# A diagonal prefix-sum kernel: more row sums on VectorE, and sixteen input rows loaded at the start

## The chip, the cores and the metric

One core of one Trainium2 chip. The metric is the device time of one execution in microseconds (us), the median over several runs. Most runs of one kernel agree within 0.3%. A version counts as the same within 2%.

## The reference

```python
def setup_inputs():
    B, H, W = 4, 4224, 4224
    return {"x": np.random.randn(B, H, W).astype(np.float32)}

def reference(x):
    ps = np.cumsum(np.cumsum(x, axis=1), axis=2)
    diag = np.diagonal(ps, axis1=1, axis2=2)
    return np.cumsum(diag, axis=1).astype(np.float32)
```

Only the diagonal of the two-dimensional prefix sum is wanted, summed up along itself. Each element of the input is needed once, as a part of a column sum or of a row sum.

## The kernel before

GpSimd issues the loads of "strips" of 768 rows, which convert fp32 to bf16 on the way. There are three strip buffers. VectorE masks the diagonal block and sums the row parts to its left; PE adds up the columns to the right, in groups of 384, six matmuls a group. For some groups VectorE adds the six rows of each partition first (`by_rows`), and PE needs one fp32 product, which it runs as two matmuls.

```python
    NBUF = 3
    ...
    head = last.tile([P, 2, HC], FP32, name="head")
    nc.sync.dma_start(out=head, in_=src_a[:, :, N - HC : N])
    ...
    for i in range(NBUF):                      # three strips on the way at once
        t = strip_tile()
        load_rows(t, 0, i * F2 * P)            # nc.gpsimd.dma_start
        prefetched.append(t)
    ...                                        # constants
    row_sums(hs[:, 0:2], head)                 # VectorE, head rows of the last batch
    ...
        def add_up(strip, f, r0, acc, um, wp=0, ws=None, by_rows=False):
            ...
            nc.vector.tensor_mul(out=mu, in0=block, in1=um)
            nc.vector.tensor_sub(out=block, in0=block, in1=mu)
            if by_rows:
                rowed = mup.tile([P, GW], FP32, name="rowed")
                row_sums(rowed, strip[:, :, hi : hi + GW].rearrange("p q c -> p c q"))
            ...                                # PE: columns of mu, product of rowed
            row_sums(acc[:, :, 1], strip[:, :, ws:hi])
```

The last 128 rows of the last batch come at the end, in four blocks of 32 rows; the last block comes in two pieces, and the sums over it end the kernel.

## Time and profile before

| | before |
|---|---|
| median of the three runs at hand | 668.94 us (667.32 to 669.8) |
| span of the profiled run | 665.6 us |
| VectorE busy | 380.8 us (57%) |
| PE busy | 206.6 us (31%) |
| from a strip load's issue to its landing | 72.6 us (median of 19) |

The span is the time from the first to the last instruction of the profiled run; the device time is some 2 us more. A row of section 5 of the page reads: line, engine, operation, what it writes from what it reads, count, then busy time and mean, then the engine's idle time just before and what ended it.

### The profile page before, as it was taken

Reading aid. Unit: us, or ns where it says so; the run is one execution under the profiler, and the core shown is the slowest. Engines: PE = TensorE matmul, PEld = TensorE weight load, DVE = VectorE, ACT = ScalarE, POOL = GpSimd, SP = SyncE. Lnnn points to the kernel's source line nnn. Section 1 sums busy time; section 2 is a strip of 40 time slices with the busy share of each in tenths; the row PEclk is TensorE's granted clock in tenths of the full one; section 3 lists DMA queues with packets and bytes.
Section 4 is the critical chain, followed back from the end, with each engine's and each line's share of the span. In section 5 each row is a group of like instructions: output and inputs, shape, how many; then the busy total and the mean of one; then the engine's idle time right before and its main releaser. Section 6 shows DMA issues by size and latency. Waiting matters only on the chain.

```text
span 665.6 us, 2495 instructions
## 1 busy us (share of the span) xinstructions
PE 206.6 (31%) x948; PEld 94.1 (14%) x948; DVE 380.8 (57%) x176; ACT 136.1 (20%) x219; POOL 31.3 (5%) x59
## 2 busy tenths in 40 slices
PE   0071522302117143140211723404031363350418
PEld 0030211100003021010000311201000131120103
DVE  3161828476946173756794526466589433352766
ACT  0001121406300103040630020304063002030434
POOL 7000000000000000000000000000000000001000
PEclk9995857656558585665655857657565585776758
DMA  9999999999999999999999999999999999999998
GB/s 203 219 219 219 219 219 218 218 209 210 219 220 219 218 220 219 218 216 215 209 219 219 219 216 219 219 218 216 213 213 219 219 216 216 219 218 218 215 206 162
DMA packets 7672, 143.23 MB, mean 215 GB/s; under 512 B 704, under 2 KB 1004, under 8 KB 2156
## 3 DMA queue, kind: packets, MB, share of 16 engines
q0 software_dynamic: 7296, 142.47, 99.9%
q1 hardware_dynamic: 364, 0.61, 0.3%
q8 instruction: 7, 0.11, 0.1%
q14 instruction: 5, 0.04, 0.0%
HBM read 285.47 MB, written 0.07 MB: 429 GB/s over the span
## 4 chain that ended last, share of the span: by engine, by line
DVE 54%; another core or an unknown queue 37%; DMA 5%; PE 3%; issue 1%; DVEq 0%; POOLq 0%
DVE acc L258 28%; DVE mu L351 8%; DVE strip L352 8%; DVE rowed L258 7%; DMA strip<-in_x_dram 5%; DVE c L481 1%; PE d L211 1%; PE fold L218 0%; PE d L218 0%; DVE pu L258 0%; DVE c L278 0%; DVE rows L403 0%; DVE acc L376 0%; PE fold_a L218 0%
## 5 line engine op out<-in xcount | busy, mean ns | idle before, releaser
L253 ACT ACTIVATE dump<-strip 128x416 bf16<-128x416 bf16 (+6 forms) x108 | 124.4, 1151 | 520.2 <-DMA strip<-in_x_dram 517.5
L351 DVE TENSOR_TENSOR mu<-strip,um 128x4608 bf16<-128x4608 bf16 (+1 forms) x24 | 52.4, 2184 | 260.4 <-DMA strip<-in_x_dram 260.3
L258 DVE TENSOR_REDUCE acc<-strip 128x6 f32<-128x4608 bf16 (+6 forms) x23 | 195.9, 8518 | 0.4
L218 PEld LDWEIGHTS <-sel 128*11 128x11 bf16 x643 | 66.7, 104 | 482.5 <-issue 453.6
L211 PE MATMUL d<-strip,sel 128*11 128x384 bf16 x90 | 37.3, 415 | 295.8 <-DMA strip<-in_x_dram 295.8
L218 PE MATMUL d<-strip,sel 128*11 128x384 bf16 x441 | 116.6, 408 | 0.0
L352 DVE TENSOR_TENSOR strip<-strip,mu 128x4608 bf16<-128x4608 bf16 (+1 forms) x24 | 52.4, 2183 | 1.0
L211 PE MATMUL d<-mu,sel 128*11 128x384 bf16 x43 | 16.3, 379 | 108.5 <-DVE mu L351 108.5
L258 DVE TENSOR_REDUCE rowed<-strip 128x384 f32<-128x2304 bf16 x12 | 49.0, 4082 | 0.0
L218 PE MATMUL d<-mu,sel 128*11 128x384 bf16 x200 | 46.7, 369 | 0.0
L76 POOL DMA_DIRECT2D strip<-in_x_dram x24 | 16.4, 686 | 542.7 <-DVE acc L258 292.8
L253 ACT ACTIVATION_READ_ACCUMULATOR dump<-strip 128x1 f32 x108 | 20.1, 186 | 0.0
L211 PE MATMUL d<-rowed,sel_f 128*11 128x384 f32 x24 | 11.5, 566 | 20.3 <-DVE rowed L258 20.3
L211 PEld LDWEIGHTS <-sel 128*11 128x11 bf16 x134 | 13.6, 102 | 19.3 <-issue 12.3
L211 PE MATMUL d<-ident,rows 128*11 128x128 f32 x24 | 5.2, 379 | 16.8 <-DVE rows L412 16.8
L258 DVE TENSOR_REDUCE pu<-d 11x1 f32<-11x384 f32 x4 | 2.2, 545 | 6.3 <-PE d L211 6.3
L94 DVE MEMSET um<- 128x4608 bf16 (+1 forms) x2 | 4.9, 2458 | 1.1 <-issue 1.1
L95 POOL TENSOR_SCALAR_AFFINE_SELECT um<-um 128x4608 bf16<-128x4608 bf16 (+1 forms) x2 | 5.2, 2612 | 2.6 <-DVE um L94 2.6
L211 PE MATMUL d<-halves,rows 128*11 128x64 f32 x48 | 5.3, 288 | 0.0
L211 PEld LDWEIGHTS d<-ident,rows 128*11 128x11 f32 x24 | 2.5, 118 | 18.9 <-DVE rows L412 11.7
L211 PEld LDWEIGHTS d<-rowed,sel_f 128*11 128x11 f32 x24 | 1.5, 91 | 24.9 <-DVE rowed L258 24.6
L211 PEld LDWEIGHTS d<-halves,rows 128*11 128x11 f32 x48 | 4.8, 128 | 1.4 <-issue 1.3
(102 smaller groups left out, 60.6 us busy)
## 6 DMA issues: line engine op xcount, KB each, us to landing
strip<-in_x_dram POOLq DMA_DIRECT2D x19, 6336.0 KB, 72.6
strip<-in_x_dram POOLq DMA_DIRECT2D x5, 3168.0 KB, 55.8
strip<-in_x_dram POOLq DMA_DIRECT2D x1, 1080.0 KB, 49.9
strip<-in_x_dram POOLq DMA_DIRECT2D x1, 768.0 KB, 52.9
strip<-in_x_dram POOLq DMA_DIRECT2D x3, 256.0 KB, 54.1
head<-in_x_dram SPq DMA_DIRECT2D x1, 528.0 KB, 3.8
strip<-in_x_dram POOLq DMA_DIRECT2D x1, 192.0 KB, 43.2
strip<-in_x_dram POOLq DMA_DIRECT2D x1, 64.0 KB, 28.5
```

The source lines that it names most:

```text
L76: nc.gpsimd.dma_start(out=o, in_=x[b, r0 : r0 + f * P, :].rearrange("(p f) w -> p f w", f=f))
L94: nc.vector.memset(um, 1.0)
L95: nc.gpsimd.affine_select(out=um, in_=um, compare_op=ALU.is_gt, fill=0.0, base=0, pattern=[[-1, f], [1, f * P]], channel_multiplier=-f,)
L211: nc.tensor.matmul(o, lhsT=lhsT, rhs=rhs, start=start, stop=False, skip_group_check=True)
L218: te.add_instruction(mybir.InstMatmult(start_tensor_calc=False, stop_tensor_calc=False, tile_position=(0, 0), tile_size=(P, P if lhsT.shap ...
L253: nc.scalar.activation(out=dump[:, :w], in_=src, func=ACT.Copy, accum_out=acc)
L258: nc.vector.reduce_sum(out=acc, in_=src, axis=AX.X)
L351: nc.vector.tensor_mul(out=mu, in0=block, in1=um)
L352: nc.vector.tensor_sub(out=block, in0=block, in1=mu)
L481: nc.vector.tensor_tensor_scan(out=c12[:, i, :], data0=ones_row, data1=src, initial=carry[:, i : i + 1], op0=ALU.mult, op1=ALU.add,)
```

## The change

The intent: take matmuls away from PE (50 groups summed on VectorE in place of 12), and shorten the end (the last 16 rows loaded at the start on SyncE's queue, behind the head and apart from the strips' queue, so that the last block has 16 rows; the 10-row store issued after a more urgent one).

```diff
+    NE = 8
+    EK = P // NE
+    EB = N - 2 * NE
+    early = last.tile([P, 2, TB // EK], FP32, name="early")
+    for h in range(2):
+        nc.sync.dma_start(
+            out=early[:, h, :],
+            in_=x[LB, EB + h * NE : EB + (h + 1) * NE, :TB].rearrange(
+                "r (k c) -> r k c", k=EK
+            ),
+        )
     ... (weights for 8 and 16 pieces a row; one "pair" tile in place of several)
+    earlysum = last.tile([P, 2], FP32, name="earlysum")
+    row_sums(earlysum, early)                  # before the loop over the batches
     ...
-            if by_rows:
-                rowed = mup.tile([P, GW], FP32, name="rowed")
-                row_sums(rowed, ...)
+            def over_rows(j0, j1):
+                rowed = mup.tile([P, 2 * GW], FP32, name="rowed")
+                ... (one reduce for two groups, then one product a group)
-                strip, F2, s * F2 * P, acc6[:, s], um6, by_rows=whole and s > 0
+            by_rows = (4, 4, 3, 2, 1) if whole else (4, 4, 0, 0, 0)
     ...
-                (3, 0, bcut),                  # last block: 32 rows, 4 pieces a row
-                (3, bcut, CB),
+                (3, RL, 8, 0, bcut),           # last block: 16 rows, 8 pieces a row
+                (3, RL, 8, bcut, CL),
     ...
+        matmul(fin_e, earlysum[:, 0:1], weights16, start=True)
+        matmul(fin_e[:, NE:], earlysum[:, 1:2], weights16[:, : R - NE])
     ...
+        store_groups()                         # the 10-row store, now after the first yl store
```

More of the change, by code (lines that the diff above doesn't have):

```diff
@@ L198, with row_weights @@
     R = P // 4
-    steps = consts.tile([P, P], I32, name="steps")
-    nc.gpsimd.iota(steps, pattern=[[4, P]], base=7, channel_multiplier=-1)
-    nc.vector.tensor_single_scalar(
-        out=steps, in_=steps, scalar=2, op=ALU.arith_shift_right
-    )
-    weights4 = consts.tile([P, P], FP32, name="weights4")
-    nc.vector.tensor_scalar_max(out=weights4, in0=steps, scalar1=0.0)
+    RL = R - 2 * NE
+    def row_weights(shift, width, skip=0):
+        k = 1 << shift
+        steps = consts.tile([P, P], I32, name="steps")[:, :width]
+        nc.gpsimd.iota(
+            steps,
+            pattern=[[k, width]],
+            base=2 * k - 1 - k * skip,
+            channel_multiplier=-1,
+        )
+        nc.vector.tensor_single_scalar(
+            out=steps, in_=steps, scalar=shift, op=ALU.arith_shift_right
+        )
+        w = consts.tile([P, width], FP32, name=f"weights{k}")
+        nc.vector.tensor_scalar_max(out=w, in0=steps, scalar1=0.0)
+        return w
+    weights4 = row_weights(2, P)
+    weights8 = row_weights(3, R)
+    weights16 = row_weights(4, R, RL)
     ident_h = consts.tile([P, P], BF16, name="ident_h")
@@ L264, in pair_sum @@
         w = src.shape[-1] // 2
-        pair = last.tile([P, 288], FP32, name=f"pair{len(pairs)}")
-        pairs.append(pair)
+        if not pairs:
+            pairs.append(last.tile([P, 288], FP32, name="pair"))
+        pair = pairs[0]
         nc.vector.scalar_tensor_tensor(
@@ L336, in columns, with add_up @@
             first[0] = False
-        def add_up(strip, f, r0, acc, um, wp=0, ws=None, by_rows=False):
+        def add_up(strip, f, r0, acc, um, wp=0, ws=None, by_rows=0):
             nw = f * P // GW
@@ L352, in add_up @@
             nc.vector.tensor_sub(out=block, in0=block, in1=mu)
-            if by_rows:
-                rowed = mup.tile([P, GW], FP32, name="rowed")
-                row_sums(
-                    rowed,
-                    strip[:, :, hi : hi + GW].rearrange("p q c -> p c q"),
-                )
             for h in range(nw):
@@ L361, in add_up @@
                     columns(g + h, 0, GW, mu[:, q, h * GW : (h + 1) * GW], q > 0)
-            if by_rows:
-                k = row_of(g + nw)
-                matmul(d, sel_f[:, NG - 1 - k : 2 * NG - 1 - k], rowed)
+            def over_rows(j0, j1):
+                rowed = mup.tile([P, 2 * GW], FP32, name="rowed")
+                n = (j1 - j0) * GW
+                row_sums(
+                    rowed[:, :n],
+                    strip[:, :, j0 * GW : j1 * GW].rearrange("p q c -> p c q"),
+                )
+                for j in range(j0, j1):
+                    k = row_of(j)
+                    matmul(
+                        d,
+                        sel_f[:, NG - 1 - k : 2 * NG - 1 - k],
+                        rowed[:, (j - j0) * GW : (j - j0 + 1) * GW],
+                    )
+            j0, j1 = g + nw, g + nw + by_rows
+            jm = min(j0 + 2, j1)
+            if jm > j0:
+                over_rows(j0, jm)
             for q in range(f):
@@ L368, in add_up @@
             row_sums(acc[:, :, 1], strip[:, :, ws:hi])
+            if j1 > jm:
+                over_rows(jm, j1)
         acc6 = smalls.tile([P, NS, F2, 2], FP32, name="acc6")
@@ L385 @@
                 load_rows(strip, b, s * F2 * P)
-            add_up(
-                strip, F2, s * F2 * P, acc6[:, s], um6, by_rows=whole and s > 0
-            )
+            by_rows = (4, 4, 3, 2, 1) if whole else (4, 4, 0, 0, 0)
+            add_up(strip, F2, s * F2 * P, acc6[:, s], um6, by_rows=by_rows[s])
             if not whole and s == 0:
@@ L437 @@
             CB = TB // 4
-            bcut = 768
-            for sb, c0, c1 in (
-                (0, 0, CB),
-                (1, 0, CB),
-                (2, 0, CB),
-                (3, 0, bcut),
-                (3, bcut, CB),
+            CL = TB // 8
+            bcut = 256
+            for sb, r, k, c0, c1 in (
+                (0, R, 4, 0, CB),
+                (1, R, 4, 0, CB),
+                (2, R, 4, 0, CB),
+                (3, RL, 8, 0, bcut),
+                (3, RL, 8, bcut, CL),
             ):
@@ L448 @@
                     out=part_b[:, sb, c0:c1],
-                    in_=x[b, r0 : r0 + R, :TB].rearrange("r (k c) -> r k c", k=4)[
+                    in_=x[b, r0 : r0 + r, :TB].rearrange("r (k c) -> r k c", k=k)[
                         :, :, c0:c1
@@ L488, with store_groups @@
             )
-        j1 = NG - t0
-        nc.sync.dma_start(
-            out=out[b, : j1 * GW].rearrange("(g i) -> g i", i=GW),
-            in_=c12[t0:NG, 1, :],
-        )
+        def store_groups():
+            j1 = NG - t0
+            nc.sync.dma_start(
+                out=out[b, : j1 * GW].rearrange("(g i) -> g i", i=GW),
+                in_=c12[t0:NG, 1, :],
+            )
         if whole:
+            store_groups()
             continue
@@ L545 @@
         )
+        store_groups()
         act_sum(bsum[:, 1, 0:1], part_b[:, 2, :448])
@@ L549 @@
             weigh_b(bsum[:, 1, i : i + 1], weights4, 2 * R)
-        act_sum(esum[:, 0:1], part_b[:, 3, :320])
-        pair_sum(esum[:, 1:2], part_b[:, 3, 320:bcut])
-        pair_sum(esum[:, 2:3], part_b[:, 3, bcut:])
+        act_sum(esum[:, 0:1], part_b[:, 3, :96])
+        pair_sum(esum[:, 1:2], part_b[:, 3, 96:bcut])
+        pair_sum(esum[:, 2:3], part_b[:, 3, bcut:CL])
         nc.scalar.copy(out=yl[:, M0:], in_=fin_b)
@@ L559 @@
         for k in (1, 0, 2):
-            matmul(fin_e, esum[:, k : k + 1], weights4[:, :R], start=k == 1)
+            matmul(fin_e, esum[:, k : k + 1], weights8)
         nc.vector.tensor_add(out=ye, in0=fin_e, in1=yl[:, E0:])
```

## The prediction

> **What bounds the kernel now.** I read the profile from the whole to the end of the span: the page's shares, its DMA rows, the waits, the stretches between strip landings, the chain of waits, and last the DMA packet records.
>
> ```profile
> span 665.6 us, 2495 instructions
> PE 206.6 (31%) x948; PEld 94.1 (14%) x948; DVE 380.8 (57%) x176; ACT 136.1 (20%) x219; POOL 31.3 (5%) x59
> DMA  9999999999999999999999999999999999999998
> q0 software_dynamic: 7296, 142.47, 99.9%
> HBM read 285.47 MB, written 0.07 MB: 429 GB/s over the span
> L351 DVE TENSOR_TENSOR mu<-strip,um 128x4608 bf16<-128x4608 bf16 (+1 forms) x24 | 52.4, 2184 | 260.4 <-DMA strip<-in_x_dram 260.3
> ```
>
> No engine is busy for more than 57% of the span, the 16 DMA engines are busy in every slice, and VectorE's first operation on a strip has waited 260 us in all for the strip to land. The bytes read, 285.47 MB, are the whole fp32 input once (4 x 4224 x 4224 x 4 = 285.47 MB), so there is nothing to save in them. The stretches between landings say the same:
>
> ```profile
> core 0: us, PE busy (x) PEld busy (x) DVE busy (x) ACT busy (x) POOL busy (x), PEclk, DMA share, GB/s
> 64.50:95.30 30.80, 11.30 (x50) 5.16 (x50) 16.14 (x4) 3.84 (x12) 0.71 (x1) 0.67 0.98 211
> 95.30:125.20 29.90, 9.49 (x39) 4.00 (x39) 18.19 (x4) 6.10 (x12) 0.56 (x1) 0.61 1.01 217
> ```
>
> A strip of 768 rows is 768 x 4224 x 4 = 12.98 MB and lands every 29.9 us, 434 GB/s, while VectorE works 10 to 20 us of it. So only four things can move the time: the rate, the start before the queue is full, the finishing times of the 16 DMA engines, and what follows the last byte. The end, from the timeline:
>
> ```profile
> 648.81 0.56 PE L211 MATMUL fold<-strip,ident_h 128*128 128x480 bf16 x1 [10.68 <-DMA strip<-in_x_dram]
> ...
> 661.57 0.41 DVE L542 TENSOR_TENSOR yl<-fin_a,c 1x256 f32<-1x256 f32 x1 [0.56 <-PE fin_a L211]
> ...
> 662.35 0.39 DVE L267 SCALAR_TENSOR_TENSOR pair<-strip 128x224 f32<-128x224 bf16 x1
> 662.69 0.29 DVE L267 SCALAR_TENSOR_TENSOR pair<-strip 128x128 f32<-128x128 bf16 x1
> ...
> 663.41 0.18 DVE L561 TENSOR_TENSOR ye<-fin_e,yl 1x32 f32<-1x32 f32 x1 [0.41 <-PE fin_e L211]
> ```
>
> Two paths end together here. One is compute: from 648.81 the chain of waits runs without a gap through PE (fold), the scans and the corner sums to VectorE at 662.3. The other is DMA: in the packet records the last piece's final completion lands at 662.67, and the last pair sum starts at 662.69. From there it is 0.9 us to the last store's issue and 2 us for that store to finish.
>
> The packet records give one more thing. Each engine keeps an exact step of 29.893 us per strip, so a delay of one engine stays to the end. At the end seven engines finish at 661.3 to 661.65 and nine at 662.3 to 662.67. What made the nine late is mostly instruction fetches: seven packets of 16,384 B on the instruction queue q8, each of which pushed one engine back by about 1.1 us, and five of 8,192 B on q14 that pushed back by 0.3 to 0.5 us.
>
> **What the Trainium skill says.** "DMA: Bandwidth & Descriptors", Where 436 GB/s comes from: 16 ports give 435.2 GB/s. The trace agrees with 434 GB/s, so I count on no higher rate. The same page, Why a DMA increments its semaphore by 16 and not by 1: a hardware-queue DMA runs on the largest k up to 16 that divides the slowest dimension of both sides, on the lowest-numbered k engines. The trace agrees in count: the 10-row store is 10 packets of 1,536 B. So the early loads (8 rows each) run on engines 0 to 7. "Runtime: NRT & Kernel Launch", Instruction fetch mechanics: instructions are refilled in 16 KiB blocks of 256. The trace agrees: the seven fetches come 124 to 132 weight loads apart, each with its matmul. "VectorE: DVE Perf Modes", The perf-mode tier table: tensor_reduce has only the 1x mode. The trace shows worse for the row sum across the six rows: 2,304 elements take 4.07 us, against 4.95 us for 4,608 elements along the free axis.
>
> **Part one, 50 groups summed on VectorE** (12 now). The row "rowed" has 12 operations of 4,082 ns, so 38 more groups are 38 x 4.08 = 155 us: VectorE goes from 381 to some 536 us. PE loses 6 matmuls of about 408 ns a group and gains 2 of 490 ns: 38 x (6 x 0.408 - 2 x 0.49) = 56 us less. VectorE's fullest strip is the second of a batch: 2 x 2.57 (mask and subtract) + 7.06 (row sum) + 4 x 4.08 = 28.5 us, under 29.9. The first takes 26.4, the third 26.4, the fourth 24.7, the fifth is unchanged. After the fifth only 15 us pass until the 3-row strip, but the following strip gives 29.9 more, as now. So the waits for strips stay. A buffer is given back up to 16 us later, at about 27 us after its landing; it is needed when the two strips queued behind it are through, at 59.8 us. Some 30 us of slack remain, and the strip time does not move. This part is worth zero by itself except through instruction fetches: 38 x (6 - 2) = 152 pairs of weight load and matmul fewer, 4 more for the early rows, 948 - 152 + 4 = 800. Fetches now come at pairs 93, 221, ... 733, 861; at 800 pairs the seventh is gone. The sixth, now at 563 us, moves to the point where 64 pairs are left, which I count back to about 654 us.
>
> **Part two, the early loads.** 2 x 131,072 B over 8 engines is 32 packets of 1 KB an engine. Packets that read 1 KB follow each other every 40.5 ns in the tail, so 1.30 us an engine. Is that hidden at the start? The head's packets run from 2.2 to 4.5 us, and on each engine the first strip's packet follows the head's last within 0.01 us. There is no idle gap behind the head, so engines 0 to 7 start the strips 1.3 us later and carry that to the end.
>
> **Part three, the 16-row block.** Now an engine has 8 packets at 117 ns and 8 at 40.5 ns, 1.26 us; after it has 16 at 40.5 ns, 0.65 us. That takes 0.61 us from all 16 engines. Net: engines 8 to 15 are 0.6 us earlier, engines 0 to 7 are 0.7 us later.
>
> **Part four, the small ones.** The 10-row store goes out at about 662.3 in place of 659.91. Its packets came after each engine's last load packet anyway, so nothing is won, and its landing stays ahead of the last store's. The early rows' sum falls in VectorE's idle 14.8 us before the first strip. Their two products (0.3 us) fit before PE's wait for the scan.
>
> **The sum.** Which engines are the late ones? The 10-row store goes to engines 0 to 9, and its packets follow each engine's last completion: six of the seven early finishers are among them and four of the nine late ones. So mostly fast engines get the extra work, which looks like a balancing. A fast engine of 0 to 7 would end at 661.3 + 0.7 = 662.0, up to 662.35; late ones above 9 at 662.65 - 0.6 = 662.05. If nothing else hit them, the last byte would land at 662.3, 0.35 earlier than 662.67. But the sixth fetch, at 654, now falls into the tail. The sixth fetch hit an engine under 10 before; if it is one of 0 to 7 (I give it 0.6) that engine ends at 661.5 + 0.7 + 1.1 = 663.3, 0.65 later. Compute follows the half strip's landing at 648.8, which engines 0 to 7 may make later by 0 to 0.4 us; a shorter pair sum gives back 0.1. So compute allows a gain of 0.1 at most. Weighted: 0.6 x 0.65 + 0.4 x 0 = +0.4 us. On the median of 668.94 that is **669.3 us**.
>
> **The rivals.** (a) Balance works: the late engines are relieved, the sixth fetch hits engine 8 or above, and the end comes when compute allows, 0 to 0.5 us earlier, 668.5 to 668.9. For it speaks that 8 engines were chosen, and that six of the fast seven lie low; against it the compute chain that has no gap. (b) VectorE becomes the bound: 28.5 us a strip is 95% of 29.9. If the 8 us sum of two groups cost 5% more, or waited for PE to have read the one buffer it writes, the second strip would run over by about 1 us; only the next one, with 3.5 us of slack, would feel it. Three whole batches would still lose nothing, as the buffers have 30 us. A loss needs VectorE over 29.9 us on average; its average is some 24. I give a loss over 2 us 0.04: 671 to 674. (c) The lighter PE gets a better clock and shortens the tail: PEclk was 0.50 between 648 and 653 us. At full clock the fold's 3.3 us would lose over 1 us. But the work taken away lies before 590 us, and the clock stood at 0.50 in 634 to 649 with PE nearly idle, so I expect none of it; even then DMA would hold the end. 668.0 to 668.6.
>
> **Range and chances.** The three runs of before spread from 667.32 to 669.8, more than any of these effects, so the range is that spread and the rivals: 667.3 to 671.0. Two per cent is 13.4 us, and 13.4 us faster would be under what the bytes need (285.47 MB at 434 GB/s is 657.8 us, with 4 us of start and 3 us of end). Faster by over 2%: 0.005. Slower needs VectorE as the bound: 0.01. Same: 0.985.
>
> **What would show it.** Right if strips still land 29.9 us apart, VectorE shows about 536 us, PE 800 matmuls, q8 six packets, the strips' time from issue to landing falls from 72.6 to about 60 us (later issue, same landing), and engines 0 to 7 show the first strip some 1.3 us after the others. Step two is wrong if the first strip starts no later on engines 0 to 7. The prediction is wrong if strips land over 30 us apart (VectorE or its traffic slows the transfers), if VectorE's waits for strips are gone, or if the tail from 648.8 to the last store shrinks by more than 1 us.

## The result and the profile after

The changed kernel takes **673.51 us** (median of 6 runs, 672.96 to 674.72) against 668.67 us (6 runs of before). The ratio is 1.0073, 95% interval 1.0058 to 1.0088. Within 2%, so "same" by that rule, but clearly slower and above the predicted range. (Ratios are the mean time of one kernel's fast runs over that of the other's of the same rounds, so not quite the ratio of the quoted medians.)

The page of the changed kernel, the same rows as shown for before:

```profile
span 671.2 us, 2223 instructions
PE 217.2 (32%) x800; PEld 80.7 (12%) x800; DVE 529.3 (79%) x197; ACT 136.0 (20%) x219; POOL 31.7 (5%) x61
DMA  9999999999899999999999999999999999999998
GB/s 204 222 220 211 217 205 217 217 217 217 171 218 219 217 218 217 217 217 217 217 216 215 217 217 217 218 217 216 217 214 217 213 217 216 217 216 217 218 210 153
HBM read 285.47 MB, written 0.07 MB: 425 GB/s over the span
L380 DVE TENSOR_TENSOR mu<-strip,um 128x4608 bf16<-128x4608 bf16 (+1 forms) x24 | 52.3, 2181 | 71.2 <-DMA strip<-in_x_dram 71.1
```

The same bytes at 425 GB/s in place of 429. Every slice but one of the first 39 moves over 200 GB/s; the eleventh of 40 moves 171. A loss in one place, then. The waits of the changed kernel show a new one (engine and line, what it waited for, us in total, times, longest):

```profile
DVE earlysum L284 <- DMA early<-in_x_dram: 45.8, 1, 45.8
POOL strip L88 <- DVE rowed L284: 324.5, 9, 75.4
```

VectorE reaches the sum of the early rows at 21.1 us and waits 45.8 us for the early load. Its timeline (start, duration, what, and in brackets the idle time before and its cause):

```profile
66.87 0.69 DVE L284 TENSOR_REDUCE earlysum<-early 128x2 f32<-128x512 f32 x1 [45.77 <-DMA early<-in_x_dram]
67.49 2.55 DVE L380 TENSOR_TENSOR mu<-strip,um 128x4608 bf16<-128x4608 bf16 x1
...
85.21 7.88 DVE L284 TENSOR_REDUCE rowed<-strip 128x768 f32<-128x4608 bf16 x1
93.00 2.55 DVE L380 TENSOR_TENSOR mu<-strip,um 128x4608 bf16<-128x4608 bf16 x1
```

In the kernel before the same multiply starts as the strip lands:

```profile
34.59 2.56 DVE L351 TENSOR_TENSOR mu<-strip,um 128x4608 bf16<-128x4608 bf16 x1 [14.81 <-DMA strip<-in_x_dram]
```

In the changed kernel the strip, landed at 35.8, lies for 32 us, and its buffer is given back only at 93.1 us. The issues of the strip loads, first before, then after (three at the start, then one as each buffer comes free):

```profile
46.14 0.77 POOL L76 DMA_DIRECT2D strip<-in_x_dram  x1 [29.56 <-PE d L218]
81.37 0.71 POOL L76 DMA_DIRECT2D strip<-in_x_dram  x1 [34.46 <-DVE acc L258]
```

```profile
93.39 0.78 POOL L88 DMA_DIRECT2D strip<-in_x_dram  x1 [75.39 <-DVE rowed L284]
121.48 0.72 POOL L88 DMA_DIRECT2D strip<-in_x_dram  x1 [27.32 <-DVE rowed L284]
147.46 0.57 POOL L88 DMA_DIRECT2D strip<-in_x_dram  x1 [25.26 <-issue]
171.70 0.70 POOL L88 DMA_DIRECT2D strip<-in_x_dram  x1 [23.66 <-DVE acc L284]
```

The three strips issued at the start are through at 94.0 us on the engines that are ahead; the fourth load is issued at 93.39 and its packets come some 2 us later. The queue runs dry for a moment. It runs dry again at the end of the batch, where a 3-row strip (15 us of transfer) takes a whole buffer: the load issued at 171.70 should have been there at 170.7. The stretches around it (length, then busy time of each engine with its count of instructions, PE's clock, DMA share, GB/s; a packet counts with all its bytes where it starts):

```profile
core 0: us, PE busy (x) PEld busy (x) DVE busy (x) ACT busy (x) POOL busy (x), PEclk, DMA share, GB/s
165.00:170.00 5.00, 0.00 (x0) 0.00 (x0) 5.00 (x1) 2.93 (x4) 0.00 (x0) 0.62 0.87 188
170.00:171.00 1.00, 0.00 (x0) 0.00 (x0) 1.00 (x2) 0.00 (x0) 0.00 (x0) 0.50 0.14 25
171.00:172.00 1.00, 0.00 (x0) 0.00 (x0) 1.00 (x2) 0.00 (x0) 0.30 (x1) 0.50 0.00 0
172.00:173.00 1.00, 0.00 (x0) 0.00 (x0) 1.00 (x1) 0.38 (x1) 0.40 (x1) 0.50 0.00 0
```

Two microseconds in which no packet starts. That is not quite two without a byte moved, as packets that began earlier still run: by the packet records the DMA engines that are ahead stand idle from 170.7 to 173.4 us, the last one for some 0.9 us. The packet records give the landings (last completion of each load, with in brackets the time from the first DMA engine's completion to the last's). Packet times in this document are put 0.3 us later than the views count them, so that a load's last completion falls on its landing in the views, 34.6 us for the first strip of the kernel before; only the changed kernel's fourth load has its landing in the views later than here, at 128.1.

| strip load | before | after | after minus before |
|---|---|---|---|
| 1st | 34.6 (0.5) | 35.8 (1.6) | 1.2 |
| 3rd | 95.3 (1.4) | 96.4 (2.4) | 1.1 |
| 4th, after the first dry spell | 125.2 (1.4) | 127.2 (1.4) | 2.0 |
| 7th, after the second | 200.0 (1.4) | 205.0 (1.0) | 5.0 |
| 13th | 364.5 (1.4) | 370.1 (1.5) | 5.6 |
| last half strip | 648.8 (1.4) | 654.4 (1.4) | 5.6 |

From the second dry spell on the changed kernel runs 5.0 to 5.6 us behind, and the end of the span is 5.6 us later (671.2 against 665.6). Note the brackets: when the queue has been empty, all 16 DMA engines start anew together, and of the 2.4 us by which some had fallen behind 1.4 are left after the first dry spell and 1.0 after the second.

Why does the early load take so long? The first of its 256 packets of 1,024 B starts at 6.03 us and the last at 66.44 us; on each of the eight DMA engines that they use they are 1.92 us apart. A strip packet (25,344 B written) takes 1.868 us (29.893 us for 16 an engine). So each engine serves the two queues in turn, one 1 KB packet against one strip packet, and 32 packets an engine wait 32 turns: 6.0 + 31 x 1.92 = 65.5 us. The head's load, on the same queue, had finished its last packets by 4.5 us, on each engine just before the first strip packet (4.1 to 4.5 us); it had nothing to take turns with.

### The profile page after: what moved, and what is told of

The parts are those of the page before. It is cut to its first block, busy times and chain, and to the rows that moved or that the text cites. A ratio compares the mean times of both kernels' runs of the same rounds, so it can differ in the third digit from the quotient of the medians.

```text
span 671.2 us, 2223 instructions
## 1 busy us (share of the span) xinstructions
PE 217.2 (32%) x800; PEld 80.7 (12%) x800; DVE 529.3 (79%) x197; ACT 136.0 (20%) x219; POOL 31.7 (5%) x61
## 4 chain that ended last, share of the span: by engine, by line
DVE 55%; another core or an unknown queue 16%; DMA 14%; issue 11%; PE 2%; POOL 2%; DVEq 0%; POOLq 0%
DVE rowed L284 26%; DMA strip<-in_x_dram 14%; DVE acc L284 13%; DVE mu L380 7%; DVE strip L381 7%; POOL um L107 1%; DVE um L106 1%; PE d L237 1%; PE fold L244 0%; PE fold_a L244 0%; DVE c L523 0%; DVE hs L284 0%; PE fin_b L237 0%; PE d L244 0%
## 5 line engine op out<-in xcount | busy, mean ns | idle before, releaser
L284 DVE TENSOR_REDUCE rowed<-strip 128x768 f32<-128x4608 bf16 (+1 forms) x28 | 198.3, 7084 | 0.0
L237 PE MATMUL d<-rowed,sel_f 128*11 128x384 f32 x100 | 68.1, 828 | 212.8 <-DVE rowed L284 212.8
L244 PEld LDWEIGHTS <-sel 128*11 128x11 bf16 x453 | 48.2, 107 | 270.0 <-issue 251.5
L244 PE MATMUL d<-strip,sel 128*11 128x384 bf16 x251 | 69.9, 425 | 0.0
L237 PE MATMUL d<-mu,sel 128*11 128x384 bf16 x43 | 16.8, 392 | 113.9 <-DVE mu L380 113.9
L237 PE MATMUL d<-strip,sel 128*11 128x384 bf16 x52 | 23.0, 443 | 92.9 <-DMA strip<-in_x_dram 92.9
L244 PE MATMUL d<-mu,sel 128*11 128x384 bf16 x200 | 48.5, 379 | 0.0
L237 PEld LDWEIGHTS d<-rowed,sel_f 128*11 128x11 f32 x100 | 9.3, 116 | 256.2 <-DVE rowed L284 234.8
L284 DVE TENSOR_REDUCE earlysum<-early 128x2 f32<-128x512 f32 x1 | 0.7, 686 | 45.8 <-DMA early<-in_x_dram 45.8
L237 PEld LDWEIGHTS <-sel 128*11 128x11 bf16 x96 | 10.7, 111 | 19.3 <-issue 14.9
## 6 DMA issues: line engine op xcount, KB each, us to landing
strip<-in_x_dram POOLq DMA_DIRECT2D x19, 6336.0 KB, 60.6
```

The costliest lines, as they stand in the source:

```text
L237: nc.tensor.matmul(o, lhsT=lhsT, rhs=rhs, start=start, stop=False, skip_group_check=True)
L244: te.add_instruction(mybir.InstMatmult(start_tensor_calc=False, stop_tensor_calc=False, tile_position=(0, 0), tile_size=(P, P if lhsT.shap ...
L284: nc.vector.reduce_sum(out=acc, in_=src, axis=AX.X)
```

## The experiments

Two theories stood. **A**: the early load lands at 66 us, VectorE waits for it with the first strip already there, and with 24 to 28 us of work in each 29.9 us it cannot catch up before the queue is empty. **B**: VectorE's 529 us of work, or its traffic, slow the kernel by themselves. A third one, **C**, is the prediction's: eight DMA engines get more work and the end waits for them. Each run is timed against before on the same chip: before was 667.6 us (7 runs) in the first group (e1 to e4) and 667.36 us (11 runs) in the second (e6 to e9). The edits are cut to what matters; e3, e6 and e9 also have the change's single "pair" tile in place of several. "The engines" that are apart or behind are the 16 DMA engines.

**e1_sum_late**: only the place of the sum moves.

```diff
-    row_sums(earlysum, early)                      # before the loop
             if not whole and s == 1:
+                row_sums(earlysum, early)          # second strip of the last batch
```

> The changed kernel, with only the sum of the early rows moved from before the first strip to the second strip of the last batch. Theory A (the early load lands only at about 66 us, VectorE waits for it until 66.9 us with the first strip already there since 35 us, and with 26 to 28 us of work a strip it cannot catch up, so the load queue runs dry at 94 and 171 us): VectorE starts the first strip at 35 us, no dry queue, 668.3 to 669.7 us. Rival B (VectorE's 529 us of busy time slow the transfers or hold the buffers): stays at 672 to 674. Rival C (8 engines get 1.3 us more at the start and the end waits for them): at most 1.5 us above before, 670.

Measured: 670.42 us (670.01 to 670.45), ratio 1.0039 (1.0024 to 1.0054). VectorE starts with the strip:

```profile
37.81 2.56 DVE L379 TENSOR_TENSOR mu<-strip,um 128x4608 bf16<-128x4608 bf16 x1 [16.71 <-DMA strip<-in_x_dram]
```

No dry spell is left in the packet records, and about 2 us of the loss of nearly 5 are gone. But 2.6 us stay (0.0039 x 667), more than A or C allowed. The records say where: the engines are 4.3 us apart from the second strip on (0.5 at that strip in before, 1.4 from the third on), and since the queue never empties, the latest one carries it on: the last half strip lands 3.1 us after before's. A holds for the dry spells; what remains fits C, if larger than I had sized it.

**e2_twelve_groups**: the change with before's 12 groups.

```diff
-            by_rows = (4, 4, 3, 2, 1) if whole else (4, 4, 0, 0, 0)
+            by_rows = (0, 1, 1, 1, 1) if whole else (0, 0, 0, 0, 0)
```

> The changed kernel with 12 groups summed over six rows as before, the early load and its sum where the change has them. Theory A: VectorE still waits until about 66.9 us, but the first buffer comes free at about 78 us in place of 93, before the queue is empty at 94 us, and VectorE catches up within two strips: no dry queue, 668.3 to 669.7 us. If the wait alone costs, whatever VectorE has to do: 671 to 673. Rival B expects before's time, too, so this run does not tell A from B; e1 and e3 do.

Measured: 669.01 us (668.91 to 671.3), ratio 1.0027 (1.0009 to 1.0045). VectorE still waits for the early rows, until 66.31 us, yet the next strip's multiply starts at 76.98 and the freed buffer's load is issued at 77.60:

```profile
66.31 0.69 DVE L284 TENSOR_REDUCE earlysum<-early 128x2 f32<-128x512 f32 x1 [45.23 <-DMA early<-in_x_dram]
77.60 0.77 POOL L88 DMA_DIRECT2D strip<-in_x_dram  x1 [59.61 <-DVE acc L284]
```

The queue is never dry. So the wait alone costs nothing at the queue; it needs the fuller strips beside it. The engines are 2.0 us apart at the second strip and 3.0 from the third on.

**e3_rows_only**: before with only the 50 groups.

```diff
-                strip, F2, s * F2 * P, acc6[:, s], um6, by_rows=whole and s > 0
+            by_rows = (4, 4, 3, 2, 1) if whole else (4, 4, 0, 0, 0)
     ... (over_rows as in the change; nothing loaded early)
```

> The kernel before with only the 50 groups (no early load, the 32-row block, the store where it was). Theory A: 668 to 669.5 us, strips 29.9 us apart, VectorE about 529 us busy. Rival B: 671 to 674. The seventh instruction fetch gone: at most 0.4 us less.

Measured: 667.8 us (667.42 to 669.27), ratio 1.0005 (0.999 to 1.002), just under the expected range. Its busy row, and the issue of its fourth strip load (93.39 us in the changed kernel):

```profile
PE 216.4 (32%) x796; PEld 80.2 (12%) x796; DVE 528.2 (79%) x192; ACT 136.1 (20%) x219; POOL 31.3 (5%) x59
61.33 0.78 POOL L76 DMA_DIRECT2D strip<-in_x_dram  x1 [44.74 <-DVE rowed L258]
```

VectorE is as busy as in the changed kernel and the time is before's. B is out. The 152 pairs fewer on PE and the instruction fetch saved are worth nothing that can be measured.

**e4_early_first**: the two early loads issued ahead of the head's.

```diff
-    nc.sync.dma_start(out=head, in_=src_a[:, :, N - HC : N])
     early = last.tile(...)
     for h in range(2): nc.sync.dma_start(out=early[:, h, :], ...)
+    nc.sync.dma_start(out=head, in_=src_a[:, :, N - HC : N])
```

> The changed kernel with the early loads issued ahead of the head load on the same queue. Theory A with its mechanism (a packet of the hardware queue gets one turn for each 25 KB packet of the strips, about 1.9 us, once strips are under way): the early rows land before 6 us, the head instead needs up to 16 turns an engine and lands at 20 to 36 us, VectorE loses at most 3 us at the first strip, no dry queue: 668.3 to 670 us. If the early load is slow because it runs on 8 engines or in 1 KB pieces, it still lands at 60 us or later, and the time stays at 673.

Measured: 675.65 us (675.22 to 676.85), ratio 1.0116 (1.0099 to 1.0133): worse, against my expectation. The waits of VectorE:

```profile
DVE hs L285 <- DMA head<-in_x_dram: 49.2, 1, 49.2
```

Now it is the head that VectorE waits for, until 68.1 us. The strips' first packets came at 3.25 us, when half of the early rows' packets were still to come, so these took turns until 35.6 us and the head's until 67.0. On an engine that has both, 16 packets of the early rows and then 16 of the head took turns, and I had counted the head's 16 alone. The mechanism is the expected one; the count was wrong. Two dry spells follow (95.2 to 99.3 and 173.9 to 177.4 us, from the first engine that stands idle to the last that starts again), longer than the changed kernel's first.

**e6_busy_no_early**: e3 with no early load, but VectorE kept busy where the changed kernel waits.

```diff
+    busy = last.tile([P, F2], FP32, name="busy")
+    for i in range(9):
+        row_sums(busy, um6)
+    for i in range(2):
+        row_sums(busy[:, :F], um3)
```

> The 50-groups kernel without an early load (e3_rows_only), with some 47 us of idle sums over a constant tile put on VectorE where the changed kernel waits for the early rows, so that it reaches the first strip at about 67 us. Theory A (the late start of VectorE together with 26 to 28 us of work a strip empties the queue): the first buffer comes free at about 92.5 us, the queue is dry at 94 and at 171 us, strips after the first batch 4 to 6 us later than in e3; 671.5 to 674 us. If the loss came from the early load's own traffic: as e3, 667.8.

Measured: 673.12 us (672.76 to 673.63), ratio 1.0078 (1.006 to 1.0097). Its timelines of VectorE and of the load issues:

```profile
19.68 47.62 DVE L258 TENSOR_REDUCE busy<-um 128x6 f32<-128x4608 bf16 x11
67.23 2.55 DVE L357 TENSOR_TENSOR mu<-strip,um 128x4608 bf16<-128x4608 bf16 x1
```

```profile
93.13 0.78 POOL L76 DMA_DIRECT2D strip<-in_x_dram  x1 [76.56 <-DVE rowed L258]
...
171.35 0.70 POOL L76 DMA_DIRECT2D strip<-in_x_dram  x1 [23.67 <-DVE acc L258]
```

The same issue times as in the changed kernel within 0.4 us, dry spells at 93.9 and at 170.2 us, and the seventh strip lands 4.8 us after before's (5.0 in the changed kernel). The changed kernel's whole loss (ratio 1.0073) is made with no early byte at all. This is the run that settles it: a late start of VectorE with the 50 groups is enough. The 11 added sums did not themselves hold up the transfers: the first three strips land at most 0.3 us after before's.

**e7_16_engines**: the early rows as one load in 2 KB pieces on all 16 engines.

```diff
-    early = last.tile([P, 2, TB // EK], FP32, name="early")
-    ... (two loads of 8 rows, 16 pieces a row)
+    early = last.tile([P, TB // 8], FP32, name="early")
+    nc.sync.dma_start(out=early, in_=x[LB, EB:N, :TB].rearrange("r (k c) -> r k c", k=8))
     ... (weights and one product to match)
```

> The changed kernel with the 16 early rows as one load of 2 KB pieces on all 16 engines (8 packets an engine in place of 32 on eight). If a packet of the hardware queue gets one turn of about 1.9 us for each strip packet, the early rows land at 4.3 + 8 x 1.95, about 20 us, before VectorE asks for them at 21 us: no wait, first strip at 35 us, no dry queue, and all engines alike: 667.0 to 669.0 us with before at 667.6 to 668.7. If bytes or the queue itself make it slow, it lands at 60 us and the time stays at 673.

Measured: 668.74 us (668.49 to 669.7), ratio 1.0013 (1.0 to 1.0027). The early load's landing time, from the view of its tile:

```profile
DMA to landing us min/median/max: 19.1/19.1/19.1
21.00 0.68 DVE L280 TENSOR_REDUCE earlysum<-early 128x1 f32<-128x512 f32 x1
```

Issued at 1.3 us and landed at 20.4; VectorE finds it there at 21.0 and never waits. The same bytes, on the same queue, three times sooner. But 8 turns made this landing on the slowest engine alone: by the packet records 13 of the 16 engines had all eight pieces by 5.7 us, directly behind the head's, and started their strips after them (the first strip packets start at 4.2 to 5.8 us, 4.0 to 4.6 in before). So this run shows more of a load that is through before the stream starts than of one that takes few turns. Why the two loads' packets came after the first strip packets and the one load's mostly before them was not looked into.

**e8_eight_engines_2k**: e7's layout in two loads of 8 rows.

```diff
-    nc.sync.dma_start(out=early, in_=x[LB, EB:N, :TB].rearrange("r (k c) -> r k c", k=8))
+    for h in range(2):
+        nc.sync.dma_start(out=early[h * 64 : (h + 1) * 64, :],
+                          in_=x[LB, EB + h * NE : EB + (h + 1) * NE, :TB].rearrange(..., k=8))
```

> The same layout as e7_16_engines, in two loads of 8 rows, so on 8 engines, 16 packets of 2 KB each. Turns: lands at 4.3 + 16 x 1.95, about 36 us, so VectorE starts the first strip at 36.5 to 38 in place of 35 and loses nothing that it can't make up; no dry queue. But engines 0 to 7 stay about 1.4 to 1.7 us behind the others to the end: 1 to 2.5 us above e7, 668.7 to 670.5 us. If the engines' lag does not matter: as e7.

Measured: 669.77 us (669.01 to 671.31), ratio 1.0029 (1.0014 to 1.0043).

```profile
DVE earlysum L283 <- DMA early<-in_x_dram: 17.6, 1, 17.6
```

It lands at 38.5 us: here all packets came after the first strip packets, and 16 on an engine make 16 turns, 2.5 us more than the 36 expected. VectorE starts the first strip at 39.3 and loses nothing at the queue. The engines are 2.4 us apart at the second strip, 1.1 in e7. The mean is about 1 us above e7's, as expected from the lag, but the two intervals overlap, so by these times alone the difference is not shown.

**e9_unused_load**: before, with the change's two early loads added and not used.

```diff
+    (the change's early loads)                     # nothing reads them
```

> The kernel before with the two early loads of the change added and their data not used (no sum, no wait, 12 groups, the 32-row block kept). Only the cost of the load on 8 engines is left: 32 packets an engine, 1.65 us on eight engines by their spread in the runs so far, 0 on the rest, carried to the end: 1.0 to 2.0 us above before. If the engines even out on the way: 0 to 0.6 us above (262 KB more at 434 GB/s).

Measured: 669.94 us (669.52 to 671.5), ratio 1.0032 (1.0017 to 1.0046): 2.1 us, just over what was expected. Here nothing waits for the load and VectorE has 12 groups; the cost is the load's own. The records show eight engines 1.5 to 2.8 us behind the first one from the second strip on, and the last piece lands 2.2 us later than before's. 262 KB more at 434 GB/s would be 0.6 us. So most of it seems to be that the bytes lie on half of the engines and that nothing evens them out; no run puts the same unused load on all 16.

No version beat the kernel before: e3 equals it, e7 is 0.13% above it by the mean, with an interval that begins at 0.

## Why the prediction was wrong

- **The bound** (the load stream; no engine near it): right. Strips land 29.9 us apart outside the dry spells.
- **Part one, 50 groups**: 529 us of VectorE (536 predicted), six fetches on q8, 60.6 us from issue to landing (about 60), and e3 shows it worth nothing. Right, except PE: predicted 56 us less, it is busy 11 us more (217.2). The sum took 408 ns for each of the 228 matmuls that go, 93 us, but these overlap one another: the matmuls on strips cover 47.5 us less of PE's time (131.5 before, 84.0 after). And the 76 more on "rowed" were put at 490 ns each, 37 us, but took 56.6 (68.1 after, 11.5 before). PE is not on the path, so this cost nothing.
- **The slack** ("Some 30 us of slack remain"): right only if VectorE starts the first strip as it lands. It was worked out for the steady state, from a start that I took for granted.
- **Part four, the step that failed**: "The early rows' sum falls in VectorE's idle 14.8 us before the first strip." I looked at the cost of the sum (0.69 us measured) and never asked when its input lands. I knew that the head, on the same queue, needs 3.8 us, and left the early load's landing time unasked; part two had its packets go by in one piece behind the head's, before the strips. They came one at a time between the strips' packets instead, the last one at 66.4 us, and VectorE, which works in program order, stood for 45.8 us. With 24 to 28 us of work in each 29.9, it won back 2 to 6 us a strip, too little for the two places where the queue was short. e6 makes the same loss out of VectorE's delay alone; e3 and e2 show that neither the 50 groups alone nor the wait alone empties the queue.
- **Part two, the early load's cost**: the lag of eight engines is right, its way and size are wrong. That "engines 0 to 7 start the strips 1.3 us later" is refuted by the prediction's own sign: the first strip packets start at 4.1 to 4.5 us on all 16, as in before (4.0 to 4.6), and the lag grows with each turn after that. The term was 1.30 us an engine. In the changed kernel eight engines fall 0.8 us behind by the first strip and 0.86 more by the second, 1.65 us in all, 51 ns a packet in place of 40.5. In e9 the whole load costs 2.1 us of time, in e1 2.6 us were left with a lag of 4.3. In the changed kernel itself this term seems to vanish in the sum, since the first dry spell lets the engines start anew together (spread 2.4 us before it, 1.4 after), and e6 has the same loss without the term. That would be why e1 recovers only about half of the loss: without dry spells the lag stays, and the two costs do not add. This is a reading of the records; no run tests it alone.
- **Part three and the tail**: the last block is shorter as worked out, and the tail's landings close part of the gap (5.7 us late at the second block of 32 rows, 5.0 us at the last piece). The last store is issued at 668.91 us, 5.3 us later than before's.
- **The rivals**: (b) came nearest, as it named VectorE and a strip sum of 95% of the transfer time, but it looked for a steady overload and dismissed a single one with "the buffers have 30 us". VectorE's delay of 32 us at the first strip used it up.

What stays open: why e1's profiled run has its engines 4.3 us apart when 1.65 us come from the packets. In it some engines started their strips up to 1 us late, and I did not separate that from the rest.

## What to carry to other kernels

Before an engine is given a sum "in its idle time", ask when the input lands, not only what the sum costs: an engine works in program order, and one early wait delays everything behind it. A small transfer beside a saturated stream of large packets is paid in turns, so count its packets on one DMA engine (few and large, over all engines: e7), place its consumer late (e1), or let it finish before the stream starts (most of e7). Slack in a buffered pipeline is one reserve for all: filling an engine to 90% of the period is free only as long as nothing delays its start.

## What the Trainium skill lacked or had wrong

- "DMA: Bandwidth & Descriptors", Queues, rings and completion order, says that an engine alternates between the queue rows with work, a packet at a time. The traces agree (1.92 us from one early packet to the next, 1.868 us for a strip packet), and I should have used it. It gives 9 to 17 descriptors as a typical packet; here each 1 KB piece took a turn of its own, 32 pieces in 60.4 us beside strip packets of 1.868 us. The page does not draw the consequence: a small load beside a saturated stream lands after (pieces per engine) x (time of one large packet), counted from its first packet: 38.5 us for 16 and 66.4 us for 32 with a start at about 6 us, and 20.4 us for 8 on e7's slowest engine.
- No page says that the DMA engines of a stream that never empties do not even out: 262 KB on eight of them came with a loss of 2.1 us (e9), while an empty queue brought the spread in the changed kernel from 2.4 to 1.4 us.
- "VectorE: DVE Perf Modes", The perf-mode tier table, has one speed for tensor_reduce; strides are not in it. Summing across the six rows of a partition took 4.07 us for 2,304 elements, along the free axis 4.95 us for 4,608: 1.6 times slower an element.
